# Moving elementwise work of q, k, v and the gated unit from GpSimd to ScalarE and VectorE in a two-layer decoder trunk

## The chip, the cores and the metric

The kernel runs on one core of one Trainium2 chip. The metric is the device time of one execution in microseconds (us). The core's engines run side by side, each on its own instruction queue: TensorE (PE, matmuls; its weight loads are listed as PEld), VectorE (DVE), ScalarE (ACT), GpSimd (POOL) and SyncE (SP, which issues the DMAs). Data lies in SBUF, in 128 partitions; matmuls write PSUM, which has eight banks of 128 x 512 float32.

## The reference

The reference is two layers of a decoder on a residual stream x of 1024 tokens by 1024 channels, all in float32. What matters for this change is the first part of a layer:

```
h = RMSNorm(x);  [u | c_q | c_kv | k_rope] = h @ w_in        # 512, 256, 128, 32 columns
y = gelu(Re(C state) + D u)                                  # diagonal state space over the tokens
y_ssm = y * sigmoid(y @ w_glu + b_glu)                       # gated unit, 512 channels
q = (rms_norm(c_q) @ w_uq)   -> 8 heads x 96
k, v = (rms_norm(c_kv) @ w_ukv) -> 8 heads x (64 + 64);  k = [k, k_rope]   # 96 wide
q, k = rms_norm(q), rms_norm(k) per head;  rope on the last 32 of the 96
y_mla = causal softmax attention(q, k, v)
x += [rms_norm(y_ssm), rms_norm(y_mla)] @ w_out
```

Behind it stand a cross-attention into 256 memory rows and a squared-ReLU MLP with 4096 hidden channels.

## The kernel before

Every float32 product on PE is made of three products of a high and a low half (type float32r): `mm3` is hi*hi + hi*lo + lo*hi. So each operand is split: ACT casts to the high half and DVE (in some places POOL) subtracts it to get the low half. Tokens go in eight tiles of 128 or two halves of 512.

The parts of a layer that the change touches, in the order in which the code is written:

- `s5_outputs` (line 1453), four calls per layer: it makes a quarter of y with matmuls and Gelu, turns it with PE transposes into channels by tokens, and stores the high half `h_` and the low half `l_`. It returns both; y itself in float32 isn't kept. It also loads two tiles, `cm` and `dm` (from `cm_d` and `kd_d` in DRAM).
- `qkv` (line 1588): for each half of the heads, eight token tiles of k and v (three matmuls of 512 columns each), then eight token tiles of q per half (six matmuls of 384 columns each). ACT moves k, the high half of v and q out of PSUM with the row's scale. The sums of squares `ssk` and `ssq` are made over two token tiles at a time: the squares of k on POOL, those of q on ACT, the sums on DVE. `rsqrt` is a series of 12 small DVE instructions (the tiles nv, nt, ssk and ssq, 32 elements wide). Then k and q are scaled by `rsk` and `scq` in place: of each half, the first four token tiles on DVE and the last four on POOL. `rope` (line 1578) multiplies by the cosine on POOL and does the rest on DVE.
- `glu` (line 1534): four column blocks of two token halves, each 12 matmuls of 512 columns into one PSUM bank, Tanh on ACT, y put together again from its halves on POOL (`sq`), (1 + tanh) * y on DVE, the split on ACT and DVE, the square on ACT, and the sum over the column blocks, `acc`, on POOL. `acc` is read only in `out_proj`.
- `attention` begins with `prep_head`: PE transposes of q and k of a head into PSUM, split by ACT and DVE.

No part runs at the place where it is written. `Program` records every operation with a rank: its place in the code plus an offset of its part, from the table `SHIFTS` (one entry per run of a part). `Program.run` then puts the operations on the engines by a list schedule with the kernel's own cost formulas (`price`), and hands out the buffers as it goes: 21 float32 tiles of 128 x 1024 (names f_..), 32 float32r tiles (r_..) and the PSUM banks (b_.. and p_..). An operation whose buffer isn't free, or whose buffer would starve one that ranks ahead, is held back. On the chip each engine then runs its queue in that fixed order. q and k take 12 of the 21 float32 tiles from their first write until attention has read them.

All operations are recorded by one helper line (721), so the profile tells them apart by engine, operation and tile names: `f<-f,ssq 128x1536` is the scaling of four token tiles of q.

Of the kernel before, what the change touches and what calls it, by code (L numbers as in the profile page):

```python
# [16 lines left out]
ALU = mybir.AluOpType  # L17
# [32 lines left out]
    "0|start|0": -7158.484375, "0|start.load_s5|0": -1830.015625, "0|prep_loads|0": -190.46875,  # L50
    "0|in_proj.first.w_in_load|0": -2.875, "0|in_proj.first.transpose_half|0": -581.90625,
    "0|in_proj.first.sumsq|0": -787.28125, "0|in_proj.first.sumsq|1": 301.859375, "0|in_proj.first.sumsq|2": -238.828125,
    "0|in_proj.first.sumsq|3": -87.828125, "0|in_proj.first.transpose_half|1": -28.25, "0|in_proj.first.sumsq|4": 167.3125,
    "0|in_proj.first.sumsq|5": -33.453125, "0|in_proj.first.sumsq|6": 82.15625, "0|in_proj.first.sumsq|7": 326.53125,
    "0|in_proj.first|0": -83.65625, "0|in_proj.first.rest|0": 539.46875, "0|in_proj|0": 497.125, "0|in_proj|1": 206.25,
    "0|in_proj|2": 29.390625, "0|in_proj|3": -6702.6875, "0|early.setup_s5|0": 33.375,
    "0|early.prep_phasors|0": -3452.53125, "0|early.prep_quarter|0": -78.640625, "0|early.prep_quarter|1": -485.1875,
    "0|early.prep_quarter|2": 61.65625, "0|early.prep_quarter|3": -21.421875, "0|setup|0": -382.03125,
    "0|s5_tokens|0": -4466.40625, "0|s5_tokens|1": -168.875, "0|s5_tokens|2": -7.296875, "0|s5_tokens|3": -8550.65625,
    "0|s5_states|1": -202.703125, "0||0": -220.796875, "0|s5_outputs|0": 243.703125, "0|s5_states|2": 43.546875,  # L60
    "0||1": -27.03125, "0|s5_outputs|1": -301.390625, "0|s5_states|3": 26.109375, "0||2": -111.5, "0|s5_outputs|2": -66.375,
    "0||3": 35.15625, "0|s5_outputs|3": 32.0625, "0|qkv|0": -6.890625, "0|qkv.rope|0": -6235.234375, "0|qkv|1": -16.703125,
    "0|qkv|2": -105.109375, "0|qkv|3": 167.28125, "0|qkv|4": -30.484375, "0|qkv|5": 377.015625, "0|qkv|6": -2.328125,
    "0|qkv|7": -2345, "0|qkv|8": 585.015625, "0|qkv.rope|1": -15.90625, "0|qkv|9": -94.078125, "0|qkv|10": 137.46875,
    "0|qkv|11": 181.96875, "0|qkv.rope|2": 1258.84375, "0|qkv|12": 252.84375, "0|glu|0": 170.125, "0|glu|1": -15.15625,
    "0|glu|2": -180.578125, "0|glu|3": -221.25, "0|glu|4": 197.4375, "0|attention.prep_head|0": -223.078125,
    "0|attention.scores|0": -230.75, "0|attention.pv|0": 131.796875, "0|attention.scores|1": -789.234375,
    "0|attention.pv|1": 143.125, "0|attention.prep_head|1": 232.9375, "0|attention.scores|2": -186.359375,
    "0|attention.pv|2": 135.3125, "0|attention.pair_done|0": 130.875, "0|attention.scores|3": -4698.03125,
    "0|attention.pv|3": 1.421875, "0|attention.prep_head|2": -110.0625, "0|attention.scores|4": 10.1875,  # L70
    "0|attention.scores|5": 1.71875, "0|attention.pv|5": 31.4375, "0|attention.prep_head|3": 89.6875,
    "0|attention.pv|6": -20.375, "0|attention.scores|7": 35.578125, "0|attention.pair_done|3": 187.203125,
    "0|attention.prep_head|4": 422.3125, "0|attention.scores|8": 53.796875, "0|attention.pv|8": 251.1875,
    "0|attention.prep_head|5": -26.796875, "0|attention.scores|10": 32.046875, "0|attention.pv|10": 111.71875,
    "0|attention.pair_done|4": 59.390625, "0|attention.scores|11": -5499.953125, "0|attention.pv|11": 48.390625,
    "0|attention.pair_done|5": 22.421875, "0|attention.prep_head|6": -78.15625, "0|attention.scores|12": -172.796875,
    "0|attention.pv|12": 92.296875, "0|attention.scores|13": 168.546875, "0|attention.pv|13": -801.359375,
    "0|attention.prep_head|7": 157.78125, "0|attention.scores|14": 124.640625, "0|attention.pv|14": -752.859375,
    "0|attention.pair_done|6": 42.640625, "0|attention.scores|15": 77.3125, "0|attention.pv|15": 47.078125,
    "0|attention.pair_done|7": -15.0625, "0|out_proj|0": -143.640625, "0|out_proj|1": 6.40625, "0|out_proj|2": 105.34375,  # L80
    "0|out_proj.branch_norm.colsum|0": 182.578125, "0|out_proj.branch_norm|0": 146.625, "0|out_proj|3": 205.5,
    "0|out_proj.prep_loads|0": 172.5, "0|out_proj.prep_phasors|0": -139.4375, "0|out_proj.prep_quarter|0": -71.84375,
    "0|out_proj|4": 507.328125, "0|out_proj.branch_norm.colsum|1": -30.046875, "0|out_proj.branch_norm|1": 861.109375,
    "0|out_proj|5": -4.75, "0|out_proj.prep_quarter|1": -1494.5625, "0|out_proj.prep_quarter|2": -64.265625,
    "0|out_proj|6": -331.984375, "0|out_proj|7": -206.75, "0|out_proj.prep_quarter|3": 261.25, "0|out_proj|8": 185.765625,
    "0|mem_kv|0": -143.140625, "0|mem_kv.sumsq|0": 153.25, "0|mem_kv|1": -486.90625, "0|mem_kv.sumsq|1": 56.421875,
    "0|mem_kv|2": 49.953125, "0|mem_kv|3": 53.5, "0|mem_kv|5": -0.359375, "0|mem_attention|0": 445.453125,
    "0|mem_attention.norm_transposed.sumsq|0": 787.171875, "0|mem_attention.norm_transposed.sumsq|1": -64.75,
    "0|mem_attention.norm_transposed.sumsq|2": -22.234375, "0|mem_attention.norm_transposed.sumsq|3": -6188.28125,
    "0|mem_attention.norm_transposed.sumsq|4": -133.640625, "0|mem_attention.norm_transposed.sumsq|5": -56.359375,  # L90
    "0|mem_attention.norm_transposed.sumsq|6": -9048.015625, "0|mem_attention.norm_transposed.sumsq|7": 185.328125,
    "0|mem_attention.norm_transposed|0": -103.40625, "0|mem_attention.norm_transposed.transpose_half|0": -491.9375,
    "0|mem_attention.norm_transposed.transpose_half|1": 405.296875, "0|mem_attention.mem_queries|0": -86.625,
    "0|mem_attention.mem_queries|1": 22.21875, "0|mem_attention.mem_queries|2": 197.109375, "0|mem_attention|1": 380.3125,
    "0|mem_attention.scores|0": 30.703125, "0|mem_attention.pv|0": -758.96875, "0|mem_attention.scores|2": -6.265625,
    "0|mem_attention.pv|1": -21.296875, "0|mem_attention.pv|2": 142.703125, "0|mem_attention.scores|4": -206.890625,
    "0|mem_attention.pv|3": -1498.34375, "0|mem_attention.scores|5": -1844.078125, "0|mem_attention.pv|4": -78.28125,
    "0|mem_attention.w_o|0": -1347.09375, "0|mem_attention.scores|6": -641.5, "0|mem_attention.pv|5": -179.453125,
    "0|mem_attention.w_o|1": -415.53125, "0|mem_attention.scores|7": -1966.171875, "0|mem_attention.pv|6": -8544.171875,
    "0|mem_attention.w_o|2": -39.453125, "0|mem_attention.pv|7": -554.125, "0|mem_attention.w_o|3": -34.953125,  # L100
    "0|mem_attention.w_o|4": 26.296875, "0|mem_attention.w_o|5": -4075.15625, "0|mem_attention.w_o|6": 10.96875,
    "0|mem_attention.w_o|7": -0.109375, "0|mlp.mlp_inputs|0": -48.9375, "0|mlp.mlp_inputs.up_load|0": -161.25,
    "0|mlp.mlp_inputs.up_load|1": -59.625, "0|mlp.mlp_inputs|1": -8.5, "0|mlp.mlp_inputs|2": 1.703125,
    "0|mlp.sumsq|0": -905.8125, "0|mlp|0": 47.4375, "0|mlp.sumsq|1": -82.421875, "0|mlp|1": -3876.859375,
    "0|mlp.sumsq|2": 338.296875, "0|mlp|2": -1122.1875, "0|mlp.sumsq|3": 417.078125, "0|mlp|3": -373.046875,
    "0|mlp|4": -7336.84375, "0|mlp.sumsq|5": 1.609375, "0|mlp|5": 60.3125, "0|mlp.sumsq|6": 804.296875,
    "0|mlp|6": 1782.4375, "0|mlp.sumsq|7": 186.234375, "0|mlp.up_split|0": -192.3125, "0|mlp.begin.up|0": -45.53125,
    "0|mlp.begin.up.up_load|0": 42.640625, "0|mlp.begin.up|1": -9.34375, "0|mlp.begin.left|0": -380.453125,
    "0|mlp.begin.up|2": -235.46875, "0|mlp.begin.up.up_load|1": -62.515625, "0|mlp.begin.up.up_split|1": -60.703125,
    "0|mlp.begin.up|3": -18.90625, "0|mlp.begin.up|4": -122.203125, "0|mlp.begin.up.up_load|2": -1824.9375,  # L110
    "0|mlp.begin.up.up_split|2": -22.890625, "0|mlp.begin.up|5": -0.21875, "0|mlp.begin.left|2": -168.453125,
# [2356 lines left out]
```

## Time and profile before

| | |
|---|---|
| median of three timed runs | 2498.59 us (2495.6 to 2498.72) |
| profiled execution, its own time | 2501.43 us |
| its span, first to last instruction | 2499.7 us |
| PE busy | 2379.1 us, 95% of the span |
| DVE busy | 1858.5 us, 74% |
| ACT busy | 1228.3 us, 49% |
| POOL busy | 366.2 us, 15% |
| mean granted clock of PE | 0.973 of full speed |

The busy shares are means over stages that have different limits: the MLP of each layer (700 to 1300 us and 1900 to 2500 us) is two long stretches of matmuls, and the stages in front of it are many short ones. The granted clock has two levels, 1.2 and 2.4 GHz; 0.973 is a mean over time. A row's idle time and the name behind its arrow tell who ended a wait. An instruction's time in the timeline runs from its start to its end, and it can start before the one ahead of it has ended.

### The profile page before, as it was taken

What the parts mean: (1) busy time and instruction counts of PE and PEld (TensorE: products, weight loads), DVE (VectorE), ACT (ScalarE), POOL (GpSimd) and SP (SyncE); (2) the same over time, 40 slices, a digit from 0 to 9 for tenths busy, and PEclk for the clock granted to TensorE, in tenths of its full rate; (3) what the DMA queues carried; (4) which work ended last, traced back from release to release, by engine and by line L of the source; (5) the groups of instructions that cost most, each with busy time, mean ns of one, the idle gap of its engine ahead of it and who ended that gap; (6) DMA issues with size and microseconds to landing.
All of it is one profiled execution on the core that took longest, in us unless ns stands there. A gap on an engine that the chain in (4) does not pass through costs nothing.

```text
span 2499.7 us, 33737 instructions
## 1 busy us (share of the span) xinstructions
PE 2379.1 (95%) x12017; PEld 1995.5 (80%) x12017; DVE 1858.5 (74%) x3456; ACT 1228.3 (49%) x2428; POOL 366.2 (15%) x332
## 2 busy tenths in 40 slices
PE   7798899999999999999999897999999999999999
PEld 6677688778678887788889886988877888888887
DVE  7879877997876666776843889884588666777783
ACT  5226677225754444443343376871466444534441
POOL 0425421231220000000000353220113000000000
PEclk9889899999999999999999998999999999999999
DMA  4351001341235236976741400051024344597671
GB/s 144 102 139 43 1 18 61 88 154 62 85 131 178 113 123 250 363 250 209 261 161 57 93 13 9 1 174 55 1 101 140 131 152 177 186 360 287 221 275 43
DMA packets 173997, 338.19 MB, mean 135 GB/s; under 512 B 32646, under 2 KB 86020, under 8 KB 173828
## 3 DMA queue, kind: packets, MB, share of 16 engines
q1 hardware_dynamic: 173828, 336.04, 39.3%
q8 instruction: 94, 1.54, 0.3%
q14 instruction: 75, 0.61, 0.1%
HBM read 246.84 MB, written 89.14 MB: 134 GB/s over the span
## 4 chain that ended last, share of the span: by engine, by line
PE 79%; DVE 13%; ACT 4%; issue 2%; DMA 2%; POOL 1%; SPq 0%; DVEq 0%; ACTq 0%; POOLq 0%
PE p L721 40%; PE b L721 39%; DVE f L721 7%; DVE r L721 4%; ACT f L721 2%; ACT r L721 2%; DVE mx L721 1%; POOL f L721 1%; DVE ssq L721 1%; DVE nt L721 0%; SPq L721 0%; DMA f<-in_x_dram 0%; DMA f<-in_mlp_w_dram 0%; DMA f<-in_w_out_dram 0%; DMA r<-h_d 0%
## 5 line engine op out<-in xcount | busy, mean ns | idle before, releaser
L721 PE MATMUL p<-r,r 128*128 128x512 f32 (+7 forms) x5508 | 1300.4, 380 | 19.4 <-ACT f L721 10.7
L721 PEld LDWEIGHTS p<-r,r 128*128 128x128 f32 (+2 forms) x5508 | 987.8, 191 | 208.1 <-ACT f L721 17.0
L721 PE MATMUL b<-r,r 128*128 128x512 f32 (+6 forms) x3868 | 954.6, 387 | 19.2 <-ACT r L721 10.0
L721 PEld LDWEIGHTS b<-r,r 128*128 128x128 f32 (+1 forms) x3868 | 723.2, 199 | 158.6 <-ACT r L721 15.1
L721 ACT CAST r<-f 128x512 fp32r<-128x512 f32 (+1 forms) x576 | 346.2, 625 | 232.2 <-PE p L721 73.6
L721 DVE TENSOR_TENSOR r<-f,r 128x512 fp32r<-128x512 f32 x512 | 355.7, 716 | 89.8 <-ACT r L721 86.1
L721 PE MATMUL b<-ident,f 128*128 128x128 f32 (+3 forms) x1371 | 226.1, 287 | 38.3 <-DVE f L721 21.1
L721 DVE TENSOR_TENSOR f<-f,f 128x512 f32<-128x512 f32 (+8 forms) x372 | 243.4, 667 | 22.3 <-ACT f L721 9.1
L721 ACT CAST r<-r 128x512 fp32r<-128x512 f32 x192 | 113.6, 618 | 239.4 <-DMA r<-h_d 179.0
L721 ACT ACTIVATE f<-f 128x512 f32<-128x512 f32 (+3 forms) x229 | 170.0, 744 | 116.1 <-DVE f L721 89.7
L721 PEld LDWEIGHTS b<-ident,f 128*128 128x128 f32 (+3 forms) x1371 | 163.1, 143 | 70.1 <-DVE f L721 23.7
L721 DVE TENSOR_TENSOR f<-f 128x512 f32<-128x512 f32 (+5 forms) x338 | 198.9, 612 | 24.7 <-DMA f<-in_mlp_w_dram 21.7
L721 DVE TENSOR_TENSOR r<-b,r 128x512 fp32r<-128x512 f32 (+1 forms) x259 | 170.1, 684 | 45.8 <-ACT r L721 44.3
L721 DVE TENSOR_TENSOR f<-b,f 128x512 f32<-128x512 f32 (+2 forms) x165 | 107.3, 662 | 101.8 <-PE b L721 74.7
L721 ACT CAST r<-b 128x512 fp32r<-128x512 f32 (+1 forms) x259 | 143.6, 591 | 73.8 <-PE b L721 59.5
L721 DVE TENSOR_TENSOR r<-r,r 128x512 fp32r<-128x512 f32 x192 | 127.5, 687 | 63.6 <-ACT r L721 48.0
L721 POOL TENSOR_TENSOR r<-f,r 128x512 fp32r<-128x512 f32 (+1 forms) x64 | 94.6, 1488 | 338.7 <-ACT r L721 300.3
L721 ACT COPY f<-b 128x512 f32<-128x512 f32 (+1 forms) x116 | 67.6, 585 | 134.7 <-PE b L721 133.7
L721 DVE TENSOR_REDUCE mx<-p 128x1 f32<-128x128 f32 (+7 forms) x128 | 94.4, 751 | 24.0 <-PE p L721 22.0
L721 ACT ACTIVATE f<-p,mx 128x128 f32<-128x128 f32 (+7 forms) x128 | 95.0, 745 | 31.0 <-DVE mx L721 27.5
L721 DVE TENSOR_TENSOR f<-p,f 128x512 f32<-128x512 f32 x99 | 67.5, 687 | 48.3 <-PE p L721 28.7
L721 POOL MEMSET f<- 128x1 f32 (+2 forms) x33 | 2.5, 108 | 679.2 <-DVE r L721 623.7
(190 smaller groups left out, 1663.1 us busy)
## 6 DMA issues: line engine op xcount, KB each, us to landing
f<-in_mlp_w_dram SPq DMA_DIRECT2D x192, 512.0 KB
h_d<-f SPq DMA_DIRECT2D x96, 512.0 KB
r<-h_d SPq DMA_DIRECT2D x96, 512.0 KB
f<-in_mlp_w_dram SPq DMA_DIRECT2D x64, 256.0 KB
x_d<-f SPq DMA_DIRECT2D x24, 512.0 KB
f<-x_d SPq DMA_DIRECT2D x24, 512.0 KB
f<-in_x_dram SPq DMA_DIRECT2D x16, 512.0 KB
f<-in_w_out_dram SPq DMA_DIRECT2D x32, 256.0 KB
```

The lines of the kernel that those rows point to most:

```text
L721: o.fn(*[a.place() if isinstance(a, View) else a for a in o.args], **{k: a.place() if isinstance(a, View) else a for k, a in o.kw.items()})
```

## The change

1. In `qkv`, the squares of k come from ACT, straight out of PSUM and one token tile at a time, in place of POOL on two tiles; the scalings of q and k are all on DVE; the cosine product of `rope` is on DVE.
2. In `s5_outputs`, ACT copies y in float32 out of PSUM into a third tile, and `glu` reads that tile in place of the sum that POOL made; the sum of squares `acc` is on DVE.
3. The table of order offsets is a new one throughout: 1009 of 1031 keys differ.

```diff
@@ SHIFTS (two of the lines) @@
-    "0|qkv|11": 181.96875, "0|qkv.rope|2": 1258.84375, "0|qkv|12": 252.84375, "0|glu|0": 170.125, "0|glu|1": -15.15625,
+    "0|qkv|11": -841.09375, "0|qkv.rope|2": 1251.34375, "0|qkv|12": -801.921875, "0|glu|0": 158.203125,
...
@@ s5_outputs @@
-        h_, l_ = r_.get(), r_.get()
+        h_, l_, y = r_.get(), r_.get(), fs.get()
...
             V.tensor_tensor(lv, pv, hv, op=ALU.subtract)
+            S.copy(y.rearrange("p (k t) -> p t k", t=8)[:, 4 * j:4 * j + 4, :], pv)
         fs.put(gt)
-        return h_, l_
+        return h_, l_, y
@@ glu @@
                 S.activation(zt[:, sl], ps, AF.Tanh, scale=0.5, bias=hb[:, l, m:m + 1])
-                G.tensor_tensor(sq[:, sl], yh[m][:, sl], yl[m][:, sl], op=ALU.add)
-                V.scalar_tensor_tensor(zt[:, sl], zt[:, sl], 1.0, sq[:, sl], op0=ALU.add, op1=ALU.mult)
+                V.scalar_tensor_tensor(zt[:, sl], zt[:, sl], 1.0, ys[m][:, sl], op0=ALU.add, op1=ALU.mult)
...
                     S.activation(sq[:, sl], zt[:, sl], AF.Square)
-                    G.tensor_tensor(acc[:, sl], acc[:, sl], sq[:, sl], op=ALU.add)
+                    V.tensor_tensor(acc[:, sl], acc[:, sl], sq[:, sl], op=ALU.add)
@@ rope @@
-        G.tensor_tensor(t1_, z, cb, op=ALU.mult)
+        V.tensor_tensor(t1_, z, cb, op=ALU.mult)
@@ qkv @@
+                sq = ta[:, 512 + (i % 2) * 256:768 + (i % 2) * 256].rearrange("p (h c) -> p h c", c=64)
+                S.activation(sq, pv[:, :, 0:64], AF.Square, scale=s2)
                 if i % 2 == 1:
-                    kk = kv4[half][:, i - 1:i + 1, :, 0:64]
-                    sq = ta[:, 0:512].rearrange("p (i h c) -> p i h c", i=2, c=64)
-                    G.tensor_tensor(sq, kk, kk, op=ALU.mult)
-                    V.tensor_reduce(ssk[:, half, i - 1:i + 1, :], sq, axis=AX.X, op=ALU.add)
+                    V.tensor_reduce(ssk[:, half, i - 1:i + 1, :], ta[:, 512:1024].rearrange("p (i h c) -> p i h c", i=2, c=64), axis=AX.X, op=ALU.add)
...
-                (V if j == 0 else G).tensor_tensor(kk, kk, rsk[:, half, ii].unsqueeze(3).to_broadcast([P, 4, 4, 64]), op=ALU.mult)
+                V.tensor_tensor(kk, kk, rsk[:, half, ii].unsqueeze(3).to_broadcast([P, 4, 4, 64]), op=ALU.mult)
...
-                (V if j == 0 else G).tensor_tensor(qv4[half][:, ii], qv4[half][:, ii],
-                                                   scq[:, half, ii].unsqueeze(3).to_broadcast([P, 4, 4, 96]), op=ALU.mult)
+                V.tensor_tensor(qv4[half][:, ii], qv4[half][:, ii],
+                                scq[:, half, ii].unsqueeze(3).to_broadcast([P, 4, 4, 96]), op=ALU.mult)
```

How the queues stand now at three places, all in the second layer. First PE, at the end of the q matmuls and the start of attention. `p_..<-r,r 128x384` are q, `b_..<-r,r 128x512` the gated unit, `<-ident,f 96x128` the transposes of q and k in `prep_head`. Before:

```order
L721 MATMUL p_34_1_4177<-r_79,r_78 128x384
L721 MATMUL p_34_1_4177<-r_87,r_78 128x384
L721 MATMUL b_112<-r_70,r_97 128x512
L721 MATMUL b_112<-r_73,r_86 128x512
...
L721 MATMUL b_112<-r_75,r_94 128x512
L721 MATMUL p_33_1_4111<-ident,f_99 96x128 x4
```

and with the change:

```order
L720 MATMUL p_33_0_4102<-r_98,r_68 128x384
L720 MATMUL p_33_0_4102<-r_83,r_94 128x384
L720 MATMUL b_112<-r_76,r_79 128x512
L720 MATMUL b_112<-r_85,r_78 128x512
...
L720 MATMUL b_111<-r_88,r_95 128x512
L720 MATMUL p_34_1_4177<-ident,f_103 96x128 x4
```

Between the last matmul of q and the first transpose stood 44 matmuls of the gated unit; now there are 71. Second, DVE at the same place: `f_..<-f_..,ssq 128x1536` is the scaling of four token tiles of q, `r_..<-p_..` the low half of q and k of the first head, and `mx` the row maximum of the first scores. Before:

```order
L721 TENSOR_SCALAR ssq<-ssq 128x32 x2
L721 TENSOR_TENSOR f_101<-f_101,ssq 128x1536
L721 TENSOR_TENSOR f_102<-f_102,ssq 128x1536
L721 TENSOR_TENSOR r_91<-p_34_0_4176,r_85 96x512
L721 TENSOR_TENSOR r_91<-p_33_1_4111,r_85 96x512
L721 TENSOR_TENSOR r_78<-f_103,r_84 128x512
L721 TENSOR_REDUCE mx_328<-p_34_1_4177 128x1
```

and with the change:

```order
L720 TENSOR_TENSOR f_103<-f_103,ssq 128x1536
L720 TENSOR_SCALAR ssq<-ssq 128x32
L720 TENSOR_TENSOR f_103<-f_103,ssq 128x1536
L720 TENSOR_TENSOR f_102<-f_102,ssq 128x1536 x2
L720 TENSOR_TENSOR r_68<-p_34_1_4177,r_91 96x512
L720 TENSOR_TENSOR r_68<-p_34_0_4176,r_91 96x512
L720 SCALAR_TENSOR_TENSOR r_94<-p_33_1_4103,gq,r_98 96x512
```

All four scalings of q stand in one row on DVE, ahead of the splits of the first head. Third, POOL over the same stage, from the scaling of k's shared rotary part (`kr,ssk`) to the first instruction of attention (`CAST r<-sm`). Before:

```order
L721 TENSOR_TENSOR f_104<-kr,ssk 128x16x32
L721 TENSOR_TENSOR f_104<-f_104,ssk 128x16x64
L721 TENSOR_TENSOR f_104<-kr,ssk 128x16x32
L721 TENSOR_TENSOR f_107<-f_102,f_100 128x1024
L721 TENSOR_TENSOR f_103<-r_75,r_82 128x512 x2
L721 TENSOR_TENSOR f_99<-kr,ssk 128x16x32
L721 TENSOR_TENSOR f_99<-f_99,ssk 128x16x64
L721 TENSOR_TENSOR f_99<-kr,ssk 128x16x32
L721 TENSOR_TENSOR f_101<-f_101,ssq 128x1536
L721 TENSOR_TENSOR f_102<-f_102,ssq 128x1536
```

and with the change:

```order
L720 TENSOR_TENSOR f_101<-kr,ssk 128x16x32 x2
L720 TENSOR_TENSOR r_78<-f_104,r_79 128x1024
L720 TENSOR_TENSOR r_95<-f_104,r_70 128x1024
L720 TENSOR_TENSOR f_99<-kr,ssk 128x16x32 x2
L720 CAST r_95<-sm_320 128x512
```

Only the rotary part of k and the split of the gated unit's weights (`r_..<-f_..,r_.. 128x1024`) are left; that split stood earlier in POOL's queue before.

## Rows read from the trace of the kernel before

**Rows 1.** Busy time of each engine by stage, with granted clock.
```profile
core 0: us, PE busy (x) PEld busy (x) DVE busy (x) ACT busy (x) POOL busy (x), PEclk, DMA share, GB/s
195.00:300.00 105.00, 86.64 (x398) 72.07 (x398) 91.49 (x169) 62.76 (x120) 59.22 (x35) 0.85 0.05 18
...
700.00:1300.00 600.00, 591.57 (x2588) 486.52 (x2589) 422.52 (x675) 268.36 (x476) 7.04 (x6) 0.99 0.58 210
1300.00:1440.00 140.00, 133.13 (x784) 125.99 (x783) 76.93 (x129) 53.96 (x131) 22.50 (x30) 0.98 0.32 79
1440.00:1535.00 95.00, 77.73 (x400) 66.53 (x399) 86.92 (x171) 62.78 (x124) 53.76 (x34) 0.89 0.02 5
...
1900.00:2499.70 599.70, 595.33 (x2617) 489.66 (x2616) 413.71 (x668) 257.65 (x461) 2.18 (x2) 1.00 0.57 204
```
**Rows 2.** Waits of PE from 195 to 300 us: total, times, longest.
```profile
PE b L721 <- DVE r L721: 5.7, 2, 3.5
PE p L721 <- DVE r L721: 5.1, 5, 1.9
```
**Rows 3.** Timeline of PE, second layer: start, us, what [idle before <-releaser].
```profile
1487.61 10.18 PE L721 MATMUL b<-r,r 128*128 128x512 f32 x44
...
1501.85 0.64 PE L721 MATMUL p<-ident,f 128*96 128x128 f32 x4 [2.06 <-POOL f L721]
1512.41 1.09 PE L721 MATMUL p<-ident,f 128*96 128x128 f32 x4 [9.91 <-DVE f L721]
```
**Rows 4.** Timeline of DVE, same place.
```profile
1492.20 2.29 DVE L721 TENSOR_SCALAR nv<-ssq 128x32 f32<-128x32 f32 x1
...
1510.60 5.98 DVE L721 TENSOR_TENSOR f<-f,ssq 128x1536 f32<-128x1536 f32 x2
```
**Rows 5.** Timeline of POOL, same place.
```profile
1492.06 2.39 POOL L721 TENSOR_TENSOR f<-f,f 128x1024 f32<-128x1024 f32 x1
...
1510.64 8.55 POOL L721 TENSOR_TENSOR f<-f,ssq 128x1536 f32<-128x1536 f32 x2 [8.84 <-DVE ssq L721]
```
**Rows 6.** POOL's groups from 195 to 300 us: xcount | busy us, mean ns | idle before.
```profile
L721 POOL TENSOR_TENSOR f<-r,r 128x512 f32<-128x512 f32 x8 | 10.6, 1340 | 2.0 <-PE b L721 2.0
L721 POOL TENSOR_TENSOR f<-f,f 128x512 f32<-128x512 f32 x6 | 9.2, 1539 | 5.5 <-ACT f L721 5.5
L721 POOL TENSOR_TENSOR f<-f 128x512 f32<-128x512 f32 x8 | 9.0, 1121 | 8.5 <-ACT f L721 4.6 <-ACT r L721 2.4 <-DVE ssk L721 1.3
L721 POOL TENSOR_TENSOR f<-f,ssq 128x1536 f32<-128x1536 f32 x2 | 8.6, 4294 | 12.8 <-DVE ssq L721 12.8
...
L721 POOL TENSOR_TENSOR f<-f,f 128x1024 f32<-128x1024 f32 x2 | 4.8, 2425 | 3.1 <-ACT f L721 3.1
L721 POOL TENSOR_TENSOR f<-f,ssk 128x1024 f32<-128x1024 f32 x2 | 4.8, 2394 | 0.0
...
L721 POOL TENSOR_TENSOR f<-kr,f 128x256 f32<-128x256 f32 x1 | 1.8, 1793 | 5.9 <-DVE nt L721 5.9
```
**Rows 7.** DVE's groups over the whole run.
```profile
L721 DVE TENSOR_TENSOR f<-f,f 128x512 f32<-128x512 f32 x256 | 178.6, 709 | 15.9 <-ACT f L721 9.1 <-DMA f<-in_mlp_w_dram 4.2
...
L721 DVE TENSOR_TENSOR f<-f,ssqm 128x1024 f32<-128x1024 f32 x4 | 4.9, 1222 | 0.1
L721 DVE TENSOR_TENSOR f<-f,f 128x1024 f32<-128x1024 f32 x4 | 4.9, 1213 | 0.0
...
L721 DVE TENSOR_SCALAR nv<-ssq 128x32 f32<-128x32 f32 x4 | 4.5, 1126 | 0.0
...
L721 DVE TENSOR_SCALAR nv<-ssqm 128x16 f32<-128x16 f32 x4 | 0.7, 170 | 0.1
```
**Rows 8.** Chain that ended last, first layer: start, us, what.
```profile
275.50 1.76 DVE f L721
```
**Rows 9.** ACT's groups over the whole run.
```profile
L721 ACT CAST r<-p 128x512 fp32r<-128x512 f32 x53 | 37.7, 774 | 18.4 <-PE p L721 18.1 <-DVE f L721 0.3
...
L721 ACT ACTIVATE f<-p,s 128x256 f32<-128x256 f32 x32 | 15.9, 496 | 3.9 <-PE p L721 2.6 <-DVE s L721 1.2
```
**Rows 10.** Waits of PE from 1300 to 1440 us.
```profile
PE b L721 <- DMA f<-kd_d: 4.1, 1, 4.1
```

More of the change, by code (lines that the diff above doesn't have):

```diff
@@ L1533, in glu @@
     @part
-    def glu(l, yh, yl, ring):
+    def glu(l, yh, yl, ys, ring):
         wgh, wgl = [], []
@@ L2417, in tile_hymba_trunk @@
         q3, k3, vs = qkv(l, rsx, cth, ctl, s12, kr, Bank(0, 1, 2, 3))
-        gh, gl, rsg = glu(l, yh, yl, Bank(4, 5, 6))
+        gh, gl, rsg = glu(l, yh, yl, [y[2] for y in ys], Bank(4, 5, 6))
         mh, ml, rsm = attention(l, q3, k3, vs)
```

615 rows, old and new, of the table SHIFTS are left out of this document.

## The prediction

> **What bounds the kernel now.** The first view is the busy time of each engine by stage. In the MLP PE is busy for 591.57 of 600.00 us in the first layer and 595.33 of 599.70 in the second [rows 1], so matmuls are the floor there. The stage of q, k, v and the gated unit is different. In the first layer (195 to 300 us) PE is busy for 86.64 of 105 us, idle for 18.4, and DVE is busy for 91.49. In the second (1440 to 1535) PE is busy for 77.73 of 95, idle for 17.3, and DVE for 86.92 [rows 1]. In both, DVE is busier than PE, ACT has about 63 us and POOL 54 to 59. The granted clock is 0.85 and 0.89 there against 0.98 to 1.00 in the other stages shown [rows 1]: part of the time it is at the lower of its two levels.
>
> The second view is PE's waits: in the first layer the two longest groups, 5.7 and 5.1 us, end with DVE [rows 2]. In the second layer the timeline shows two gaps between the gated unit's matmuls and the first transposes of attention: 2.06 us ended by POOL and 9.91 us ended by DVE's scaling of q [rows 3]. So the queue of DVE ends the idle time, and the question is what slows it.
>
> The third view sets DVE's timeline beside POOL's. DVE's instruction on the 32-element tile nv takes 2.29 us, from 1492.20, and POOL's rope product runs from 1492.06 for 2.39 us [rows 4, 5]. Over the run this instruction has a mean of 1126 ns; the same operation in cross-attention (`nv<-ssqm`, 16 elements) has 170 ns [rows 7]. Two scalings of q on DVE take 5.98 us while POOL does its own two in 8.55 [rows 4, 5]; one without a neighbour took 1.76 [rows 8]. So in this trace DVE stretches when POOL reads at the same time.
>
> The Trainium skill says the same (SBUF — State Buffer, "Who interferes with whom"): GpSimd's ports are DVE's shared second pair, held for a whole instruction, and a DVE instruction with two SBUF inputs contends with GpSimd's reads. The 2.29 against 0.17 us agrees. By that rule alone nearly all of POOL's removed time could be DVE's gain, and the sum would lie at the PE floor, about 2463; the q scalings, which lost far less, speak against that much.
>
> **The change part by part.** POOL, per layer: 10.6 (y from its halves) + 9.2 (six of `acc`) + 9.0 (squares of k) + 8.6 (scalings of q) + 4.8 (rope) + 4.8 (scalings of k) + 1.8 (rope of the shared part) = 48.8 us leave [rows 6].
>
> DVE, per layer, gets two rope products at 1.21 = 2.4 and two scalings of k at 1.22 (the nearest row is `f<-f,ssqm`, same size) = 2.4 [rows 7]; two scalings of q at 1.76 = 3.5 [rows 8]; six `acc` sums at 0.71 = 4.3 [rows 7]; the small rope product, a quarter of a large one, about 0.4. Together 13.0 us.
>
> DVE, per layer, loses its stretching. No single row has the total, so I take it from two pairs: beside POOL's 8.55 us two scalings lost 5.98 - 2 x 1.76 = 2.46, a share of 0.29; beside POOL's 2.39 us nv lost 2.29 - 0.17 = 2.12, a share of 0.89. On 48.8 us that is 14 or 43 us; the lower bound is nv alone over the run, 4 x (1126 - 170) = 3.8, or 1.9 per layer. I take 14, since most of what leaves POOL is large products like the scalings. Net, DVE's queue in this stage is about 1 us shorter. It is not shorter work that I expect to help, but where it falls: the stretched small instructions are a chain that must end before q can be scaled, while `acc` is read only in `out_proj` and can stand late.
>
> ACT, per layer, gets 16 squares of k at 0.50 = 7.9 us and eight copies of y at 0.77 = 6.2 [rows 9]. The copies fall in the state-space stage, where ACT is busy for 53.96 of 140 us [rows 1]: nothing. The squares fall in a stage where ACT has 63 of 95 to 105 us; they stand between the moves of k and v out of PSUM, so I charge 1 us (bounds 0 and 7.9). Without the slack each would delay the freeing of a PSUM bank.
>
> *Second layer.* The waits to win are 2.06 + 9.91 = 12.0 us [rows 3]. Before, 44 matmuls of the gated unit, 10.18 us, stood between q's last matmul and the first transpose [rows 3]; now 71 stand there, at 10.18 / 44 = 0.231 us each 16.4 us, so the cover is 6.2 us longer. DVE's chain up to the scaling changes by its share of the relief, taken as 8.8 of the 14, less one pair of k scalings and one of rope products (4.8): 4.0 shorter. Against that all four scalings of q stand in one row, 7.0 us instead of 5.98: 1.0 longer. Together 6.2 + 4.0 - 1.0 = 9.2 of the 12.0. ACT takes 1 back, and I add 1.5 for the clock: with fewer gaps PE spends less of this stage at the lower level. Result: -10 (bounds +3, if relief is 1.9 and the cover is merely matmuls taken from an earlier gap; and -17.3, all of PE's idle time). What is late next is the transposes' own split on DVE, which stands behind the four scalings.
>
> *First layer.* PE is idle for 18.4 us, in many short waits [rows 1, 2]. The two DVE groups are 10.8 of it; I take three quarters, 8, and 1 for the clock: -9 (bounds 0 and -18.4).
>
> *Everything else.* No matmul is added or removed, but the whole order is new, which moves every buffer and load. I price that at 0. Its width comes from the two MLP stretches, the same work in two orders: 8.4 and 4.4 us idle, 4 apart [rows 1]; over four such stages, two of them independent in sign, ±8.
>
> The sum is -10 - 9 + 0 = -19. Against the profiled execution's own time, 2501.43 us, that is 2482.4. The median of the runs is 2.84 us below that execution, so the forecast for the median is 2479.6, say **2480 us**; own range 2468 to 2492 (the ±8, with ±9 on the two layers' terms, added as independent).
>
> **The rivals.**
>
> *A, slower: DVE becomes the bound.* DVE has 86.92 of 95 us in the second layer's stage [rows 1] and gets 13.0. If the stretching that goes is only about 6 us, because most of it lay where DVE would have waited for PE or ACT anyhow, the stage's DVE work is 94 us, and every microsecond beyond is PE's wait: +7 per layer, 2498.6 + 14 = about 2512. It decides as soon as relief is below 13.0. For it: relief is a guess between 1.9 and 43. Against it: 4.3 of the 13 can leave the stage, and the pairs in [rows 4, 5] alone account for 4.6 us in some 25 us of one layer. Chance 0.10. The Trainium skill takes this side (Perfetto Trace Analysis, "Optimizing Scalar/DVE Operations"): where DVE is saturated, some of its work may go to Scalar or even GPSIMD, which is the reverse of this change; but it adds that moves between DVE and GPSIMD might not help, as they share a port. The stretched rows agree with the second half.
>
> *B, no change: the new tiles starve loads.* y now holds four of the 21 tiles from the state-space stage to the gated unit, while q and k take 12. The loads of `cm` and `dm` need two tiles for each call, so they start later. One such wait is there already, 4.1 us of PE for a tile from `kd_d` [rows 10]. If two of the four calls in each layer wait that long, 4 x 4.1 = 16.4 us are given back: 2479.6 + 16.4 = 2496. For it: five tiles are left. Against it: q and k are first written after this stage, and PE there is busy for 133.13 of 140 us [rows 1]. Chance 0.13.
>
> *C, more: the stages fall to the PE floor.* If DVE's relief is nearer to the 43, PE's idle 18.4 + 17.3 = 35.7 us vanish nearly whole: 2498.6 - 35.7 = 2463. For it: the 2.29 us row, and a higher clock on top. Against it: other waits of PE in these stages are for PSUM, whose readers are ACT and DVE with more work than before. Chance 0.13.
>
> **How the numbers follow.** The forecast has 0.64, C 0.13, B 0.13, A 0.10. About 0.2%, 5 us, is what a measurement here can tell from no change: faster is below 2493.6, slower above 2503.6. Faster holds C and nearly all of the forecast (0.13 + 0.61) and a fifth of B (0.03): 0.77. Same holds 0.02 of the forecast and most of B (0.10): 0.12. Slower holds A and a tail of the forecast (0.11). The range of 8 in 10 leaves out A and half of C with the tails: 2466 to 2499.
>
> **What would show it.** In the profile after, POOL should be busy for about 98 us less. `nv<-ssq` should fall from 1126 to near 170 ns: if it stays above 500, the relief is wrong. In the second layer's stage PE's wait ahead of the first transposes should be 2 to 4 us instead of 12.0; if it is still DVE's and longer than 8, cover or chain was wrong. DVE's busy time of that stage should be 82 to 90 us; near 95, with PE waiting for DVE, is A. PE waits for `cm_d` or `kd_d` above 10 us a layer are B. PE idle below 8 us in both stages is C. The stages outside should keep their lengths within 2 us each; a difference beyond 8 in their sum, of whatever sign, means that the new order and not the moved work made the result, and would overturn the forecast, as would ACT's squares ending PE's waits for PSUM.

## The result and the profile after

The changed kernel takes 2520.78 us (median of 4 runs, 2517.64 to 2524.6) against 2498.48 us before: a ratio of 1.0093, 95% interval 1.0075 to 1.011. It is slower by 22 us; the forecast was 2480 us, faster by 19. The profiled execution took 2520.38 us; its span of 2518.6 is 18.9 us longer than that of before.

To see where, both traces are cut at four points at which both orders have done practically the same work. The points are counts of matmul records of PE (1708, 3560, 5976 and 7330 of 12,017). A reaches to the middle of the first layer's attention, B to its MLP's first matmuls, C is that MLP, D runs from the end of C to the first scores of the second layer's attention (state space, q, k, v, gated unit), E is the rest up to the last matmul. Lengths in us, one profiled execution each, the kernels of the experiments with them:

| kernel | A | B | C | D | E | median of its runs |
|---|---|---|---|---|---|---|
| before | 368.2 | 349.9 | 560.5 | 267.8 | 949.3 | 2498.48 |
| changed | 357.4 | 374.2 | 549.9 | 265.1 | 968.1 | 2520.78 |
| e1 moves, order of before | 382.4 | 348.8 | 561.1 | 278.8 | 954.4 | 2528.23 |
| e12 work of before, new order | 375.3 | 374.3 | 550.4 | 276.2 | 965.4 | 2548.06 |
| e3 joint of two orders, first try | 355.3 | 355.2 | 550.7 | 298.2 | 968.7 | 2534.79 |
| e5 order of before in B | 359.4 | 349.8 | 550.3 | 264.8 | 965.5 | 2494.29 |
| e6 order of before in B and E | 358.4 | 352.7 | 550.1 | 262.6 | 958.1 | 2482.98 |
| e7 scalings, rope and acc alone | 370.0 | 347.3 | 561.7 | 269.1 | 951.3 | 2503.98 |
| e8 squares of k alone, from PSUM | 382.5 | 349.5 | 560.5 | 275.7 | 948.1 | 2524.68 |
| e9 squares of k alone, from SBUF | 369.6 | 348.0 | 560.0 | 269.4 | 954.6 | 2506.28 |
| e10 as e6, squares from SBUF | 357.1 | 350.0 | 550.1 | 260.2 | 950.6 | 2475.02 |
| e11 as e10, squares on POOL | 359.4 | 351.3 | 551.4 | 265.4 | 950.7 | 2484.88 |

E also differs between kernels that have the same order and the same work there: before, e1, e7, e8 and e9 have 948.1 to 954.6 us. So a few us in E say nothing. And the runs of the kernel before that were taken beside the experiments have medians of 2496.86 to 2501.0 us, so kernels of different sets are compared by their ratio to before.

The changed kernel gains 10.8 us in A, 10.6 in C and 2.7 in D, and loses 24.3 in B and 18.8 in E: 19 us in all. The view of busy time by stretch (columns as in [rows 1]; the last row goes on to the end of the span), first the kernel before:

```profile
0.00:368.20 368.20, 310.66 (x1708) 266.30 (x1708) 303.65 (x692) 183.36 (x385) 123.39 (x127) 0.92 0.27 76
368.20:718.10 349.90, 331.57 (x1854) 270.36 (x1854) 294.95 (x624) 186.58 (x393) 91.23 (x76) 0.97 0.27 86
718.10:1278.60 560.50, 552.43 (x2417) 454.41 (x2416) 402.02 (x650) 254.11 (x452) 0.11 (x1) 0.99 0.60 217
1278.60:1546.40 267.80, 243.66 (x1356) 220.56 (x1355) 181.33 (x328) 130.54 (x281) 76.40 (x64) 0.95 0.20 53
1546.40:2499.70 953.30, 940.77 (x4687) 783.85 (x4685) 676.58 (x1167) 473.66 (x918) 75.09 (x64) 0.99 0.43 152
```

and the changed kernel:

```profile
0.00:357.40 357.40, 303.24 (x1708) 258.98 (x1708) 296.23 (x703) 196.93 (x409) 71.37 (x98) 0.94 0.27 78
357.40:731.60 374.20, 340.15 (x1854) 277.53 (x1854) 293.26 (x626) 187.12 (x396) 93.66 (x76) 0.95 0.25 79
731.60:1281.50 549.90, 548.87 (x2417) 452.86 (x2417) 399.81 (x646) 249.86 (x446) 0.00 (x0) 1.00 0.62 220
1281.50:1546.60 265.10, 247.87 (x1356) 220.80 (x1355) 175.38 (x344) 145.91 (x309) 31.23 (x36) 0.95 0.19 57
1546.60:2518.60 972.00, 945.92 (x4687) 787.64 (x4685) 683.79 (x1167) 472.81 (x919) 75.30 (x64) 0.99 0.42 149
```

B is the row to look at: 374.2 us long with PE busy for 340.15, so PE is idle for 34.1 us; before it was idle for 18.3. The other 8.6 of the 24.3 us are PE's busy time. No operation of B is touched by the change, and DVE, ACT and POOL do there what they did (293, 187 and 94 us; before 295, 187 and 91).

Inside the stage of q, k, v the steps came out nearly as forecast. PE in the second layer, to be read against [rows 3]:

```profile
1489.32 16.30 PE L720 MATMUL b<-r,r 128*128 128x512 f32 x71
1507.81 0.65 PE L720 MATMUL p<-ident,f 128*96 128x128 f32 x4 [2.20 <-DVE f L720]
...
1509.56 1.52 PE L720 MATMUL p<-ident,f 128*96 128x128 f32 x12 [0.67 <-DVE f L720]
```

The 71 matmuls take 16.30 us, and the waits of 2.06 and 9.91 us have become 2.20 and 0.67; behind them stands one of 1.63 us for ACT's high half. DVE's groups over the whole run, against [rows 7, 8]:

```profile
L720 DVE TENSOR_TENSOR f<-f,ssq 128x1536 f32<-128x1536 f32 x8 | 13.9, 1753 | 0.0
L720 DVE TENSOR_TENSOR f<-f,ssk 128x1024 f32<-128x1024 f32 x8 | 12.8, 1628 | 0.2 <-DVE nt L720 0.2
L720 DVE TENSOR_SCALAR nv<-ssq 128x32 f32<-128x32 f32 x4 | 0.7, 172 | 0.0
```

`nv<-ssq` fell from 1126 to 172 ns, the scalings of q are all at 1.75 us, and only the scalings of k, which still run beside POOL's rotary products of k, are longer than estimated (1.63 against 1.22 us). POOL's groups from 195 to 300 us, against [rows 6]:

```profile
L720 POOL TENSOR_TENSOR f<-kr,ssk 128x512 f32<-128x512 f32 x4 | 5.1, 1296 | 32.1 <-DVE ssk L720 32.1
L720 POOL TENSOR_TENSOR r<-f,r 128x1024 fp32r<-128x1024 f32 x2 | 4.8, 2411 | 2.3 <-ACT r L720 2.3
```

And PE's wait for `kd_d` from 1300 to 1440 us, against [rows 10], which speaks against rival B (in the first layer there is now one such wait, of 3.3 us, where there was none):

```profile
PE b L720 <- DMA f<-kd_d: 1.8, 1, 1.8
```

PE's three longest groups of waits in B are these, before and then changed (total, times, longest):

```profile
PE b L721 <- DVE f L721: 6.3, 8, 1.9
PE b L721 <- DVE r L721: 4.3, 9, 1.4
PE b L721 <- ACT f L721: 2.7, 4, 1.0
```
```profile
PE b L720 <- DVE f L720: 12.1, 6, 5.6
PE p L720 <- ACT f L720: 7.0, 9, 2.8
PE b L720 <- ACT f L720: 6.5, 8, 1.8
```

All groups together, the waits that DVE ends went from 11.4 to 18.3 us and those that ACT ends from 6.4 to 15.3. The longest single wait is at the start of cross-attention in the first layer. PE of the changed kernel:

```profile
560.82 11.19 PE L720 MATMUL b<-r,r 128*128 128x512 f32 x48
577.62 1.73 PE L720 MATMUL b<-ident,f 128*128 128x128 f32 x7 [5.60 <-DVE f L720]
```

and DVE there, the scaling of the memory's keys, the last of a chain of small instructions that starts when the 48 matmuls of `mem_kv` give their result:

```profile
576.78 0.69 DVE L720 TENSOR_TENSOR f<-f,rsk 128x512 f32<-128x512 f32 x1
```

The same place in the kernel before, PE and then DVE:

```profile
565.23 7.56 PE L721 MATMUL p<-r,r 128*128 128x512 f32 x32
572.77 1.94 PE L721 MATMUL b<-ident,f 128*128 128x128 f32 x16
```
```profile
571.98 0.69 DVE L721 TENSOR_TENSOR f<-f,rsk 128x512 f32<-128x512 f32 x1
```

Before, 32 matmuls of the output projection stood beside that chain, and PE went on without a wait. In the new order the output projection is done when `mem_kv` runs, nothing covers the chain, and PE waits for 5.60 us. That is a third of what B lost in idle time; the rest is spread over many waits, which were not followed one by one. The granted clock of B is 0.95, and was 0.97 before.

### The profile page after: what moved, and what is told of

Its sections match the earlier page's. It is cut to its first block, busy times and chain, and to the rows that moved or that the text cites. A ratio compares the mean times of both kernels' runs of the same rounds, so it can differ in the third digit from the quotient of the medians.

```text
span 2518.6 us, 33673 instructions
## 1 busy us (share of the span) xinstructions
PE 2386.1 (95%) x12017; PEld 1997.8 (79%) x12017; DVE 1848.5 (73%) x3482; ACT 1252.6 (50%) x2476; POOL 271.6 (11%) x274
## 5 line engine op out<-in xcount | busy, mean ns | idle before, releaser
L720 PE MATMUL p<-r,r 128*128 128x512 f32 (+8 forms) x5460 | 1307.4, 381 | 42.4 <-ACT f L720 19.8
L720 PE MATMUL b<-r,r 128*128 128x512 f32 (+5 forms) x3916 | 962.4, 385 | 11.0 <-DVE r L720 5.4
L720 PEld LDWEIGHTS b<-r,r 128*128 128x128 f32 (+1 forms) x3916 | 731.8, 199 | 149.5 <-DVE r L720 11.5
L720 DVE TENSOR_TENSOR r<-f,r 128x512 fp32r<-128x512 f32 x512 | 349.6, 704 | 103.5 <-ACT r L720 90.7
L720 DVE TENSOR_TENSOR f<-f,f 128x512 f32<-128x512 f32 (+8 forms) x392 | 258.2, 672 | 26.9 <-DMA f<-in_mlp_w_dram 15.8
L720 PE MATMUL b<-ident,f 128*128 128x128 f32 (+3 forms) x1371 | 228.2, 291 | 47.0 <-DVE f L720 24.1
L720 DVE TENSOR_TENSOR f<-f 128x512 f32<-128x512 f32 (+8 forms) x334 | 195.5, 605 | 27.2 <-DMA f<-in_mlp_w_dram 18.9
L720 POOL TENSOR_TENSOR r<-f,r 128x512 fp32r<-128x512 f32 (+1 forms) x64 | 94.8, 1492 | 409.6 <-ACT r L720 267.8
L720 DVE TENSOR_TENSOR f<-p,f 128x512 f32<-128x512 f32 x98 | 66.7, 689 | 57.7 <-PE p L720 34.1
L720 DVE SCALAR_TENSOR_TENSOR r<-f,gcol,r 128x512 fp32r<-128x512 f32 (+3 forms) x86 | 60.4, 733 | 63.8 <-ACT r L720 63.7
```

The source lines that it names most:

```text
L720: o.fn(*[a.place() if isinstance(a, View) else a for a in o.args], **{k: a.place() if isinstance(a, View) else a for k, a in o.kw.items()})
```

## The experiments

In most of them the list schedule is replaced by a list, which leaves the rest of the kernel as it was:

```diff
-    def run(self, trace=None):   # list schedule: ranks, costs, buffers that come free
+    def run(self, trace=None):   # k > 0: issue operation k; k < 0: it is done, its buffers come free
+        for k in ORDER:
```

ORDER is the sequence in which one of the two kernels issues its operations. An operation that exists in both keeps its place, a new one stands behind its neighbour in the code.

**e1, the moves alone.** All moves but the float32 y, whose four tiles have no room in the old order.

```diff
-ORDER = (from the new table)
+ORDER = (that of the kernel before)
-    V.scalar_tensor_tensor(zt[:, sl], zt[:, sl], 1.0, ys[m][:, sl], op0=ALU.add, op1=ALU.mult)
+    G.tensor_tensor(sq[:, sl], yh[m][:, sl], yl[m][:, sl], op=ALU.add)
+    V.scalar_tensor_tensor(zt[:, sl], zt[:, sl], 1.0, sq[:, sl], op0=ALU.add, op1=ALU.mult)
```

> The moved work of q, k, v and of acc (scalings, rope, squares of k, acc) in the order of before, operation by operation; y is still put together on POOL, since the four extra tiles do not fit into that order. Theory T (the new order loses the time outside the stage, the moved work gains): 2480 to 2490 us, the two stages 5 to 10 us shorter each, everything else as before. Rival R (the moved work itself costs the time, by a later DVE and tiles held longer): 2500 us or more, with PE's waits for DVE in the two stages as long as before or longer.

Measured: 2528.23 us, ratio 1.0107 (1.0088 to 1.0126). R's number, and against T: the moves alone cost 14.2 us in A and 11.0 in D and leave B, C and (but for 5 us) E as they were. That holds for this order only: in the changed kernel A and D are shorter than before.

**e2 and e12, the order alone.**

```diff
-ORDER = (that of the kernel before)
+ORDER = (that of the changed kernel; POOL's sums and squares behind their neighbours)
```

> The work of before (POOL keeps all that it had) in the order of the changed kernel. Theory T: slower than the changed kernel or equal to it, 2520 to 2535 us, with the loss between the end of the first layer's attention and its MLP (about 22 us) and in the second layer's same part (about 10). Rival R: about 2498 us, as before.

> The work of before in the order of the changed kernel once more, with POOL's squares of k behind the writes that they read (in the earlier run nine of these sums stood ahead of them, so that its output differed there). Theory T: 2535 to 2550 us as in the earlier run; outside the two stages every part as long as in the changed kernel. Rival R: under 2520 us.

In e2 nine of POOL's operations stand ahead of the writes that they read, in e12 none, so e12 is the one to go by. Measured: 2547.15 us for e2, and for e12 2548.06 us, ratio 1.0194 (1.0175 to 1.0212). As T said. B and E of e12 are as long as in the changed kernel (374.3 and 965.4), though nothing of the moved work is in it: that loss is the order's. So is the gain in C (550.4). Its A and D are longer than in either kernel, so the new order gains there only with the moved work. Two rows of e12, B and D (columns as in [rows 1]):

```profile
375.30:749.60 374.30, 340.98 (x1853) 277.78 (x1854) 293.18 (x625) 187.18 (x396) 93.88 (x76) 0.95 0.25 79
...
1300.00:1576.20 276.20, 245.24 (x1355) 220.23 (x1354) 176.57 (x331) 132.55 (x285) 75.49 (x65) 0.95 0.18 55
```

**e3 and e4, joining two orders, first try.**

```diff
-ORDER = (new)
+ORDER = (new, to the end of attention 0) + (before, to the middle of up projection 0) + (new)       # e3
+ORDER = (as e3, to the end of attention 1) + (before)                                               # e4
```

> The changed kernel, with the order of before from the end of the first layer's attention to the middle of the first layer's up projection, and the new order elsewhere. Theory T: the first layer's part from attention to MLP takes about 22 us less, 2499 us in all. Rival R (tiles and work of the change push this part late): the part keeps its length, 2518 us or more.

> As the one with the old order in the first layer's output projection and cross-attention, and in addition the order of before from the end of the second layer's attention to the end. Theory T: 10 to 15 us less again, 2484 to 2490 us, faster than both kernels. Rival R: 2515 us or more.

Measured: 2534.79 us (1.0137, 1.0121 to 1.0152) and 2532.79 us (1.0127, 1.0112 to 1.0142). By the number it is R, but not for R's reason: B did come back (355.2 us in both), and D grew to 298.2 and 296.7 us. The way of joining is the likely cause: the tiles then lay in other places, and an operation that finds no tile or bank free at its turn is issued later. In the list of e3 at least 288 operations of the second layer stand elsewhere than in that of e5. So D of these two says nothing of the change.

**e5 and e6, joined where both orders have issued the same.** Each operation also gets the buffer that it has in its own order, where that is free; 10 and 17 operations had to be held back.

```diff
-ORDER = (new)
+ORDER = (new, to the middle of attention 0) + (before, to the first matmuls of up projection 0) + (new)  # e5
+ORDER = (as e5, to the first scores of attention 1) + (before)                                           # e6
```

> The changed kernel, with the order and the buffer places of before from the middle of the first layer's attention to the first matmuls of its up projection; new order elsewhere, joined where the two orders have issued the same operations but for 4 to 6. Theory T (the new order loses the time from the first layer's attention to its MLP): the 23 us lost there (3.4 + 5.9 + 14.2) come back, 2497 to 2501 us, and all other stages keep their lengths. Rival R (that part is longer because of what the moved work leaves behind): 2518 us or more, that part as long as in the changed kernel. Rival S (any joint of two orders disturbs what follows, as in the earlier joint): the second layer's stage of q, k, v takes 105 us or more instead of 95.

> As the one before, and the order of before also from the second layer's attention to the end. Theory T: another 3 + 10 + 5 us come back, 2479 to 2486 us, faster than both kernels. Rival R: 2515 us or more. Rival S: 2500 us or more, with longer stages behind the joints.

Measured: e5 2494.29 us, ratio to before 0.9974 (0.9964 to 0.9984); e6 2482.98 us, 0.9932 (0.9914 to 0.9951). T's number for e6, 3 us below it for e5; R and S are out. B of e5:

```profile
359.40:709.20 349.80, 329.84 (x1854) 269.07 (x1854) 294.53 (x626) 186.88 (x395) 91.17 (x76) 0.98 0.28 89
```

349.8 us instead of 374.2, with the same work on every engine and the clock at 0.98.

**e7 to e9, which of the moves costs.** All in the order of before.

```diff
 # e7: as the change has them: scalings of q and k, rope, acc on DVE
 # e8: as the change has it
+                S.activation(sq, pv[:, :, 0:64], AF.Square, scale=s2)        # 16 per layer, from PSUM
 # e9: in the place of POOL's square
-                    G.tensor_tensor(sq, kk, kk, op=ALU.mult)
+                    S.activation(sq, kk, AF.Square)                          # 8 per layer, from SBUF
```

> The kernel before, in its own order, with the scalings of q and k, the rope product and acc on DVE; the squares of k and the sum of y stay on POOL. Theory P (ACT's squares of k hold PSUM banks longer and cost the 25 us of the earlier run): 2490 to 2502 us. Rival D (the scalings in DVE's queue cost them): 2512 to 2525 us, with 12 us or more of waiting ahead of the second layer's first transposes.

> The kernel before, in its own order, with the squares of k alone moved to ACT. Theory P: 2510 to 2522 us, with PE waiting for ACT's moves out of PSUM in the first layer's stage. Rival D: 2490 to 2502 us.

> The kernel before, in its own order, with each of POOL's 16 squares of k done by ACT in the same place, from SBUF and over two token tiles, so that no PSUM bank waits for a square. Theory B (in the run with the squares straight from PSUM the 24 us came from banks that were freed later, behind a longer chain on ACT): 2496 to 2504 us, PE's waits for ACT in the stage of k and v as before. Rival L (ACT's added 6 to 8 us per layer are themselves the cost): 2510 us or more.

Measured: e7 2503.98 us (1.0014, 1.0005 to 1.0024), e8 2524.68 us (1.0098, 1.008 to 1.0116), e9 2506.28 us (1.0039, 1.0024 to 1.0053). D is out, though P was 2 us too low for e7 and 3 for e8: the scalings cost next to nothing in the old order, although PE waits 13.25 us there ahead of the second layer's first transposes. The squares from PSUM make up most of the cost of e1 (22.2 of 25.2 us in A and D). PE's longest group of waits in the first layer's stage, e8 and then e9 (total, times, longest):

```profile
PE p L1256 <- ACT f L1256: 15.7, 8, 4.3
```
```profile
PE p L1255 <- ACT f L1255: 5.0, 2, 4.3
```

With the squares from PSUM PE waits 15.7 us for ACT, eight times; from SBUF 5.0, twice. In A and D e9 is 3.0 us longer than before, e8 22.2. The likely cause is the PSUM bank: it can't take the next tile of k and v until ACT has come to the square. It isn't shown alone, since e9 also has half as many squares, and 7.8 us more of ACT's time than before where e8 has 12.2. e9's time lies between the two numbers expected. Its profiled execution is 5.8 us longer than that of before, and 5.3 of them are in E (954.6), where neither work nor order differs. The granted clock of cross-attention (1772 to 1905 us) is 0.88 in this execution, and was 0.93 before; whether all runs have that stays open.

**e10 and e11, the better version.**

```diff
 # e10: e6 with
-                S.activation(sq, pv[:, :, 0:64], AF.Square, scale=s2)
+                    S.activation(sq, kv4[half][:, i - 1:i + 1, :, 0:64], AF.Square)      # every second tile
 # e11: the same on POOL
+                    G.tensor_tensor(sq, kk, kk, op=ALU.mult)
```

> The version with the old order in the middle parts (2483 us) with the squares of k from SBUF over two token tiles, at the place of every second square. Theory B: the new order already leaves room for the squares from PSUM (PE idles 12 us in each stage there), so 2478 to 2484 us, at most a few us less. Rival L: 2483 to 2488 us, no gain.

> The 2475 us version with the squares of k back on POOL, from SBUF over two token tiles, at the same place of the order; all else the same. Theory C (POOL's squares stretch DVE by 0.3 to 0.9 of their 9 us per layer, and DVE ends this stage): 2478 to 2490 us, the stretch back in DVE's small instructions. Rival N (in this order it no longer matters who makes the squares): 2473 to 2478 us.

Measured: e10 2475.02 us, ratio 0.9913 (0.9898 to 0.9928), less than expected and the fastest of all. Its interval overlaps that of e6, and in the profiles A and D, where the squares are, are only 1.3 and 2.4 us shorter than in e6, so what the squares from SBUF gave is not clear. e11 2484.88 us, 0.9937 (0.9919 to 0.9955): C's number; its interval overlaps that of e10 a little. In the profiles e11 is 5.2 us longer in D. DVE of e11 at one of POOL's squares of the second layer, and POOL at the same time:

```profile
1446.33 1.01 DVE L1255 TENSOR_TENSOR nt<-ssk 128x32 f32<-128x32 f32 x1
```
```profile
1446.25 1.04 POOL L1255 TENSOR_TENSOR f<-f 128x512 f32<-128x512 f32 x1 [3.14 <-DVE r L1255]
```

The small instruction takes 1.01 us, as long as the square; the five others like it in this stage take 0.19. The stretch comes back. It is not all of the 5.2 us: in the same stage DVE's sums also wait for POOL's squares, where in e10 they wait 0.9 us for ACT's:

```profile
DVE ssk L1255 <- POOL f L1255: 2.9, 3, 1.9
```

E of e10 is near its old length, 950.6; e6's 958.1 comes from an execution that took 4.6 us more than the median of e6.

## Why the prediction was wrong

- **Everything else: 0 ± 8.** This is the step that failed. B, C and E together came out at +32.5 us (24.3 - 10.6 + 18.8). The bound was read from PE's idle time in the two MLP stretches, 8.4 and 4.4 us. It failed even there: the new order takes 10.6 us out of C, with either work, since a wait of PE that was most of those 8.4 us is gone:

```profile
PE b L721 <- ACT r L721: 6.9, 1, 6.9
```

The loss lies mainly between the MLPs: all of B's 24.3 us, and 13.6 of E's 18.8, in the part ahead of the second MLP (365.0 us before, 378.6 now). e12 shows that it is the new order's with the old work, e5 and e6 that it goes with the old order and the new work. Why each wait there is longer stays open but for the chain at `mem_kv`. The prediction named no rival for it: its rivals were all waits or work of the change itself. It did name the sign, a difference beyond 8 us outside the two stages.

- **POOL and DVE.** Right. POOL's busy time fell by 94.6 us (366.2 to 271.6; 97.6 forecast). DVE's, with 26 us of work added at the forecast's prices, fell from 1858.5 to 1848.5 us, so by this sum some 36 us of stretching went over both layers; 28 were forecast. In the Trainium skill (SBUF — State Buffer, "Who interferes with whom") the shared port is the reason; 1126 against 172 ns agrees. One reading was wrong: the scaling of 1.76 us did have a neighbour, POOL's own scaling, which began 0.05 us behind it:

```profile
275.50 1.76 DVE L721 TENSOR_TENSOR f<-f,ssq 128x1536 f32<-128x1536 f32 x1
275.55 4.33 POOL L721 TENSOR_TENSOR f<-f,ssq 128x1536 f32<-128x1536 f32 x1 [2.44 <-DVE ssq L721]
```

So DVE isn't stretched whenever POOL runs. In the rows here it is stretched where it begins second: `nv<-ssq` began 0.14 us behind POOL's product [rows 4, 5], the 1.01 us instruction of e11 0.08 us behind POOL's square. The price of 1.76 holds, since the scalings take 1.75 with no POOL scaling left. The Trainium skill (Perfetto Trace Analysis, "Optimizing Scalar/DVE Operations") allows that work goes from a saturated DVE to Scalar or even GPSIMD, with the doubt that the shared port may undo it; here the doubt decides, since DVE took POOL's work and was busy for less.

- **Second layer's wait.** The mechanism was right: cover 16.30 us (16.4 forecast), the waits of 12.0 us down to 2.9. The size was not: D is 2.7 us shorter, not 10. The 9.1 us won there are 6.9 in all of D's idle time (24.1 to 17.2), since other waits grew, and the recorded busy time of PE for the same 1356 matmuls rose by 4.2 (243.66 to 247.87); why, the runs don't show.
- **First layer.** Forecast -9; A is 10.8 shorter, and nearly all of it lies in the stage itself. Some 450 matmuls of it, before and then changed:

```profile
203.90:314.90 111.00, 92.70 (x453) 78.01 (x452) 94.54 (x157) 71.73 (x142) 55.17 (x33) 0.88 0.03 10
204.30:304.60 100.30, 87.27 (x454) 72.25 (x452) 90.48 (x174) 77.89 (x157) 9.92 (x6) 0.97 0.01 4
```

The number was right in part by luck. Of the 10.7 us, 5.3 are idle time, where 8 were forecast from the waits for DVE, and 5.4 are PE's busy time at a granted clock of 0.97 instead of 0.88, where 1 was forecast. The waits for DVE that were to go are 8.8 us of these rows now, and were 9.7.

- **ACT's squares: 1 us, bounds 0 and 7.9.** Not contradicted in the new order (A and D of e6 are 1.3 and 2.4 us longer than with squares from SBUF, e10). In the old one they cost 14.3 us in A and 7.9 in D (e8): in the first layer nearly twice the upper bound, which counted ACT's time and not the bank that the square holds. The prediction had the words ("delay the freeing of a PSUM bank") and no price.
- **Rivals.** A (DVE the bound): no, DVE in the second layer's stage (1440 to 1535 us) fell from 86.92 to 84.28 us. B (late loads): no, 1.8 us instead of 4.1 in the second layer and 3.3 instead of none in the first, against the 10 us a layer that were its sign. C: no, PE still idles for 12.2 of those 95 us.

Work and order are not two terms that add. Against the runs of before beside them the moves alone (without y) cost 27 us (e1) and the order alone 47 (e12), and both together 22; in A and D they gain together what neither gains by itself. What is left over is the order's loss in B and E, less its gain in C.

## What to carry to other kernels

When a change brings a whole new order, don't price the order at nothing, and don't read its width from one kind of stage. Go through the stages that the change doesn't touch, and ask at each chain of small instructions which matmuls stand beside it. Work that reads PSUM can cost more than its own time: the squares of e8 are 12.2 us more on ACT and 22.2 us more in A and D. If a new order gains in one stage and loses in another, join the two orders where both have issued the same operations, and let each keep its own buffers.

## What was not expected of the hardware

One 0.48 us square on ACT per tile of k and v turned PE's waits for ACT from 3.8 us (kernel before, first layer's stage) into 15.7. And an order replayed with other places for its tiles is another program: e3 and e5 were to run the second layer in the same order, and D took 298.2 and 264.8 us.
